# A hybrid trunk step in fp32: seven block products for the mixer's last projection and for three tile pairs of the attention's last one, and an earlier swap of a small-tile pool

## The chip, the cores and the metric

The kernel runs on one core of a Trainium2 chip. The metric is the device time of one execution in microseconds, as the median of several runs; lower is better. One further execution is recorded by the hardware profiler.

## The reference

One layer of a trunk is applied to 512 prompt tokens and 64 sample tokens with a state of their own, D = 1024, all in fp32:

```python
x = x + mixer(rmsnorm(x))        # gated delta net || gated linear attention
x = x + cross_attn(rmsnorm(x), mem_k, mem_v)
x = x + conv_ffn(rmsnorm(x))     # up, causal conv of width 3, SiLU gate, down
y = rmsnorm(x)
```

The parts that the change touches are these:

```python
merged = sigmoid(gt_a) * (o_a @ w_out_a) + sigmoid(gt_b) * (o_b @ w_out_b)
mixer  = merged @ w_o                                   # "wo"
m = rmsnorm(mem); k = m @ w_mk; v = m @ w_mv            # 256 memory tokens
a = softmax((h @ w_mq) @ k.T / 16)                      # 4 heads of 256
cross_attn = concat_heads(a @ v) @ w_mo                 # "mo"
ffn = (silu(conv(h @ w_up_gate)) * conv(h @ w_up_val)) @ w_down   # D_FF = 2816
```

The new memory keys and values, the recurrences' states and the last rows of both convolutions are outputs too.

## The kernel before

**Arithmetic.** TensorE multiplies in a reduced fp32 format. To reach fp32, weights and activations are each split into a high part and a low rest, and each block product is three matmuls: high times high, high times low, low times high. A projection tile of 128 outputs has 8 blocks of 128 inputs, and each block streams all 576 tokens (256 and 320 columns): 8 x 3 x 2 = 48 matmuls. Its accumulator is a tile `big` of two PSUM banks, of which there are two; four single banks are called `sm`.

**Weights.** SP fetches a raw tile of 512 KB (`wr`, three of them). ACT writes its rounded copy to the high tile and the negative of that to the low tile, and POOL issues a DMA that adds the raw weights to the low tile from HBM (`w<-wt`, `w<-wd` for the down projection). `fetch` prefetches in the fixed order `WORDER` as long as weight tiles `w` are free: six (`WB`) in the first part of the kernel, and six more (`WF`) from a pool `fp`.

**Order.** A planner (`Driver`) keeps a clock and a cost for each operation and writes the instructions of each engine in the order that comes out of it. All of them are issued from one line, so that the profile gives one line for nearly everything, L227, and groups go by the names of tiles. On the chip each engine takes its instructions in that order and waits on semaphores. The same order is written for PE, and prefetched weights fall into the gaps of the other engines' plans.

**Stages.** In order of PE's work: the input projections with the two recurrences in between (to about 345 us); 16 gate tiles; 8 tiles `out` (418.7 to 469.6 us), whose results are gated and merged, split into `mgh` and `mgl`; 8 tiles `wo` (469.6 to 520.4 us), each added to a tile of x that is loaded again just before; then the memory keys `mk`, values `mv` and queries `mq` with the attention of four heads; 8 tiles `mo` (the first six blocks of tiles 0 and 1 fill the last head's softmax, the rest runs from 663.8 to 705.4 us), each followed by the sum of squares and the split for the next norm; 44 tiles `up` with the convolution and gating beside them; and the down projection.

**Block products.** The down projection doesn't run as plain tiles. The 22 blocks of 128 inputs are cut into parts of six (the last of four). For a part and a pair of neighbouring output tiles, the weights are a 2 x 2 matrix of quarters, a11 to a22, and the activations (even and odd block, first and second half of the 576 tokens) another. Seven products of sums of quarters take the place of eight, in a variant of Strassen's method: P1, P2, P3, Q4, Q5, Q6, Q7. `emit_product` makes the sums of the weights (`ws`, on DVE), `operands` those of the activations (`tu`, `tw`), and `products` runs the matmuls of 288 columns into `sm` banks and adds or subtracts each result into the two halves of x by DVE. The blocks stand at 803 to 837, 915 to 948 and 1026 to 1059 us, each with four pairs; the last part follows the last `up` tile.

**Pools.** The small tiles of the recurrences live in a pool `tp`. It is closed, and `fp` opened in its place, in `main` after `mo` and before the first `up`:

```python
        drv.flush(float("inf"))
        tctx.close()
        nonlocal tp, fp
        tp = fp = ctx.enter_context(tc.tile_pool(name="fp", bufs=WF))
        drv.spawn(c_rstat("n3", [(acc, 0)], 4, True, 2.0))
```

`c_rstat` makes a norm's row factor and copies it to all partitions (`rbc`); `up` results are multiplied by it when DVE takes them out of PSUM (`fu<-big,rbc`).

Of the kernel before, what the change touches and what calls it, by code (L numbers as in the profile page):

```python
# [17 lines left out]
P = 128  # L18
# [9 lines left out]
NS = 57  # L28
RAWB = 3
WB = 6  # L30
WF = 6
# [17 lines left out]
M_ID, M_TRI, M_NEG, M_N1, M_ONE, M_GLA, M_SH, M_LEV = 0, 128, 256, 384, 512, 640, 768, 896  # L49
# [12 lines left out]
def weight_order():  # L62
    seq = list(HEADS)
    for m in range(8):
        seq += [("gta", m), ("gtb", m)]
    seq += [("out", m) for m in range(8)]
    seq += [("wo", m) for m in range(8)]
    for hd in range(4):
        seq += [("mk", 2 * hd), ("mk", 2 * hd + 1)]
        if hd % 2 == 0:  # L70
            seq += [("mv", 2 * hd + i) for i in range(4)]
        seq += [("mq", 2 * hd), ("mq", 2 * hd + 1)]
    seq += [("mo", m) for m in range(8)]
    for kd, i in FFN:
        if kd == "up":
            seq += [("up", i), ("up", NJ + i)]
        elif kd == "dns":
            seq += [("dn*", u) for u in product_order(i)]
        else:
            seq += [("dn", (m, 3)) for m in i]  # L80
    return seq
# [6 lines left out]

PRODUCTS = ("P1", "Q5", "Q6", "P2", "P3", "Q7", "Q4")


def product_order(pairs):
# [23 lines left out]
WFULL = [w for w in WORDER if w[0] not in ("dn", "dn*")]  # L116
# [79 lines left out]
class Driver:  # L196
# [32 lines left out]
    def where(self, ap):  # L229
# [4 lines left out]
        if ap.space == bass.MemoryType.PSUM:  # L234
            return ap.tensor.name, (0, P, 0, 1024)
# [20 lines left out]
    def rotate(self, tag, bufs, tile_):  # L256
# [3 lines left out]
        if len(q) >= bufs:  # L260
            end, old = self.free_at(tag)
            q.remove(old)
# [151 lines left out]
def tile_trunk(ctx, tc, xT, memT, wt, wd, vec, cst, w0, wgate, st_gdn, st_conv, st_gla, st_ffn, ckT, cv,  # L414
# [57 lines left out]
    def raw_tile():  # L472
        return keep(drv.rotate("raw", RAWB, wp.tile([P, 1024], F32, tag="raw", name=nm("wr"), bufs=RAWB)))
# [11 lines left out]
    def emit_weight(i):  # L485
        kind, idx = WORDER[i]
        if kind == "dn*":
            wready[i] = emit_product(*idx)
            return
# [23 lines left out]
    halves_of = {}  # L513

    def emit_product(pair, prod):

        m, p = pair
        n = len(PARTS[p]) * 64
        if prod == "P1":
            r = halves_of[pair] = []  # L520
            for i in range(2):
                raw = raw_tile()
                c0 = PART0[p] * 128
                src = wd[m + i, :, c0:c0 + 2 * n]
# [5 lines left out]
        def total(a, b):  # L530
            s_ = slot("ws")
            V.tensor_tensor(s_[:, 0:n], a, b, op=ALU.add)
            r.append(s_[:, 0:n])
            return s_[:, 0:n]

        src = {"P1": lambda: a11, "Q5": lambda: total(a21, a22), "Q6": lambda: total(r[4], a11), "P3": lambda: total(r[5], a12),
               "Q7": lambda: total(a11, a21), "P2": lambda: a12, "Q4": lambda: a22}[prod]()
# [7 lines left out]
        if prod in ("P2", "Q4"):  # L545
            drop(src)
# [15 lines left out]
    def fetch(i):  # L562

        room = WB + (WF if fp is not None else 0)
        for j in range(i, len(WORDER)):
            if j in wready:
                continue
            if len(drv.pending & wnames) + (1 if WORDER[j][0] == "dn*" else 2) > room:
# [12 lines left out]
    cst_t = cp.tile([P, NM], F32, name="cst")  # L581
# [12 lines left out]
    w0_t = cp.tile([P, 256], F32, name="w0")  # L594
    DMA(w0_t, w0)
    ident = cst_t[:, M_ID:M_ID + 128]
    tri = cst_t[:, M_TRI:M_TRI + 128]
    neg = cst_t[:, M_NEG:M_NEG + 128]
    negm1 = cst_t[:, M_N1:M_N1 + 128]
    ones = cst_t[:, M_ONE:M_ONE + 128]  # L600
    shift = cst_t[:, M_SH:M_SH + 128]
    glam = cst_t[:, M_GLA:M_GLA + 128]
# [8 lines left out]
    wg_t = cp.tile([P, 256], F32, name="wg")  # L611
    cst_in = cp.tile([P, 12, 3], F32, name="cstin")
    cst_out = cp.tile([P, 12, 6], F32, name="cstout")
    csamp = cp.tile([P, 12, TS], F32, name="csamp")
# [124 lines left out]
    sg = cp.tile([P, 12, 20], F32, name="sg")  # L739
# [16 lines left out]
    def c_gates(ba):  # L756
        G.memset(bt, 0.0)
        p1 = sm()
        sel = cst_t[:, M_SEL:M_SEL + 8]
# [145 lines left out]
    def c_gdn(h):  # L905
# [118 lines left out]
        for li, b in enumerate(LEVELS):  # L1024
# [10 lines left out]
            lm = cst_t[:, M_LEV + 128 * li:M_LEV + 128 * li + 128]  # L1035
# [253 lines left out]

    def c_att(hd):  # L1290
        ks_, vs_, kp_, vp_ = N["ks", hd], N["vs", hd], N["k", hd], N["v", hd]
# [45 lines left out]
        for j in range(2):  # L1337
# [15 lines left out]
        drv.done.add(("att", hd))  # L1353


    def main():
# [53 lines left out]
        DMA(cst_t, cst)  # L1410
# [88 lines left out]
        mg = []  # L1499
        for m in range(8):  # L1500
# [8 lines left out]
            h, lo = slot("mgh", F32R), slot("mgl", F32R)  # L1509
            A.copy(h[:, 0:T], g0[:, 0:T])  # L1510
            X.tensor_tensor(lo[:, 0:T], g0[:, 0:T], f(h[:, 0:T]), op=ALU.subtract)
            mg.append((h, lo))

        def res_finish(ps, m, scale, gcol, acc_, out):
            for xx, i in zip(two(x[m]), pv(ps)):
                V.scalar_tensor_tensor(xx, i, scale, xx, op0=ALU.mult, op1=ALU.add)
            out.append(norm_prep(x[m], vcol(gcol + m)))
            sq_acc(acc_, x[m], m == 0)

        acc = slot("acc")  # L1520
        out = []
        for m in range(8):
            xt = slot("x")
            DMA(xt[:, 0:T], xT[:, m, :])
            x[m] = xt
            b = []
            yield from tile_proj("wo", m, xs_of(mg), b)
            res_finish(b[0], m, 0.5, C_GMEM, acc, out)
        xs = xs_of(out)
        drv.spawn(c_rstat("n2", [(acc, 0)], 4, True, 2.0))  # L1530

        first = True
        yield ("nm",)
        N["mrt"], N["mbc"] = N["nm"]
        for hd in range(4):
            kr = slot("kraw")
            for j in range(2):
                wh, wl = weight("mk", 2 * hd + j)
                ps = big()
                for k in range(KT):  # L1540
                    a, b = N["mx"][k]
                    mm3([(ps[:, 0, 0:256], slice(0, 256))], wh, wl, a, b, k, k == 0, k == 7)
                    if k % 2:
                        yield 0.7
                V.tensor_tensor(kr[:, 256 * j:256 * j + 256], ps[:, 0, 0:256], N["mbc"][:, 0:256], op=ALU.mult)
            DMO(o_mk[256 * hd:256 * hd + 256, :].rearrange("(j p) t -> p j t", p=P), r4(kr[:, 0:512], 256))
            N["k", hd] = split(kr)
            ckr, cvr = slot("ckr"), slot("cvr")
            DMA(r4(ckr[:, 0:512], 256), ckT[:, 2 * hd:2 * hd + 2, :])
            DMA(r4(cvr[:, 0:512], 256), cv[:, 256 * hd:256 * hd + 256].rearrange("(a p) d -> p a d", p=P))  # L1550
            N["ks", hd], N["vs", hd] = split(ckr), cvr
            if hd % 2 == 0:
                nh = hd // 2
                vr = [slot("vraw") for _ in range(2)]
                ps = big()
                for kp in range(4):
                    wh, wl = weight("mv", nh * 4 + kp)
                    for tt in range(2):
                        c = slice(128 * tt, 128 * tt + 128)
                        for k in range(2):  # L1560
                            a, b = N["mx"][2 * kp + k]
                            w1, w2 = wh[:, 512 * k:512 * k + 512], wl[:, 512 * k:512 * k + 512]
                            PE.matmul(ps[:, tt, :], a[:, c], w1, start=(kp == 0 and k == 0), stop=False)
                            PE.matmul(ps[:, tt, :], a[:, c], w2, start=False, stop=False)
                            PE.matmul(ps[:, tt, :], b[:, c], w1, start=False, stop=(kp == 3 and k == 1))
                            yield 1.0
                for tt in range(2):
                    for j in range(2):
                        A.activation(vr[j][:, 256 * tt:256 * tt + 256], ps[:, tt, 256 * j:256 * j + 256],
                                     AF.Identity, scale=N["mrt"][:, tt:tt + 1])  # L1570
                for j in range(2):
                    DMO(o_mv[:, 256 * (hd + j):256 * (hd + j) + 256].rearrange("(a p) d -> p a d", p=P), r4(vr[j][:, 0:512], 256))
                    N["v", hd + j] = split(vr[j])
            for j in range(2):
                m = 2 * hd + j
# [413 lines left out]
```

## Time and profile before

| | |
|---|---|
| median of 3 runs | 1142.08 us (1141.47 to 1143.43) |
| the profiled execution | 1141.34 us, span 1139.5 us |
| 8 tiles `wo` | 469.6 to 520.4 us |
| `mo` after the last head | 663.8 to 705.4 us |
| first `up` tile | from 705.4 us |
| DMA | 172.53 MB, mean 151 GB/s |

The page gives for each engine its busy time, the share of the span and the number of instructions. A row of a group gives line, engine, operation, tiles written and read, count, busy time, mean nanoseconds of one, and the idle time before them with what ended it. A row of the timeline gives start, duration, engine, operation, and in brackets the idle time ahead of it. A row of the chain of waits gives start, duration, engine and tile.

### The profile page before, as it was taken

The numbers are of one execution on the slowest core, as the hardware profiler recorded it, in microseconds if no ns is written. First come the engines' busy times: TensorE is split into PE (matmuls) and PEld (weight loads), VectorE is DVE, ScalarE is ACT, GpSimd is POOL, SyncE is SP. The second block draws the span as 40 slices with busy tenths as digits, with TensorE's granted clock in tenths as the row PEclk, the third lists the DMA queues.
The fourth block names the chain that finished last, engine by engine and source line by source line (L and its number), as shares of the span: only waits on it lengthen the run. The fifth ranks groups of instructions, "written<-read, shape, count | busy, mean of one in ns | idle before, by whom it ended". The sixth has DMA issues, their size and how long they took to land.

```text
span 1139.5 us, 21399 instructions
## 1 busy us (share of the span) xinstructions
PE 1117.0 (98%) x8453; PEld 1076.4 (94%) x8453; DVE 628.7 (55%) x1296; ACT 618.3 (54%) x1138; POOL 294.8 (26%) x540
## 2 busy tenths in 40 slices
PE   8999999999999999999999999899999999999997
PEld 7899989998889999999999999899999999999987
DVE  6777646555533135345563443467835773677475
ACT  6766437554534354454545555654646555656554
POOL 4244114521311131111001011324423342343332
PEclk9999999999999999999999999999999999999999
DMA  8665334654336678885836846974697579848834
GB/s 259 149 144 126 63 79 89 153 121 101 80 65 166 173 171 199 224 178 141 230 120 156 205 110 156 230 181 74 141 257 178 100 165 224 208 73 189 189 68 122
DMA packets 61557, 172.53 MB, mean 151 GB/s; under 512 B 7056, under 2 KB 19600, under 8 KB 61456
## 3 DMA queue, kind: packets, MB, share of 16 engines
q0 software_dynamic: 25632, 73.41, 37.8%
q1 hardware_dynamic: 35824, 97.74, 26.2%
q8 instruction: 67, 1.10, 0.4%
q14 instruction: 34, 0.28, 0.1%
HBM read 163.13 MB, written 5.37 MB: 148 GB/s over the span
## 4 chain that ended last, share of the span: by engine, by line
PE 93%; DVE 3%; ACT 2%; DMA 1%; issue 0%; SPq 0%; POOL 0%; ACTq 0%
PE big L227 70%; PE sm L227 22%; DMA wr<-wt 1%; ACT w L227 1%; DVE x L227 1%; DVE fc L227 0%; DVE c L227 0%; SPq L227 0%; ACT xh L227 0%; DVE acl L227 0%; ACT sq L227 0%; DVE xl L227 0%; DVE gy L227 0%; DVE w L227 0%; DVE gna L227 0%
## 5 line engine op out<-in xcount | busy, mean ns | idle before, releaser
L227 PE MATMUL big<-xh,w 128*128 128x256 f32 (+1 forms) x3072 | 554.8, 300 | 6.7 <-DMA wr<-wt 3.9
L227 PEld LDWEIGHTS big<-xh,w 128*128 128x128 f32 x3072 | 463.1, 189 | 13.1 <-issue 8.8
L227 PE MATMUL big<-xl,w 128*128 128x256 f32 (+1 forms) x1536 | 330.3, 297 | 1.8 <-DVE xl L227 1.8
L227 PEld LDWEIGHTS big<-xl,w 128*128 128x128 f32 x1536 | 259.2, 190 | 2.4 <-DVE xl L227 2.4
L227 POOL DMA_DIRECT2D w<-wt x118 | 103.3, 882 | 445.4 <-ACT w L227 411.9
L227 ACT ACTIVATE w<-wr 128x1024 fp32r<-128x1024 f32 (+3 forms) x164 | 148.6, 906 | 109.8 <-PE big L227 52.9
L227 ACT CAST w<-wr 128x1024 fp32r<-128x1024 f32 (+3 forms) x184 | 164.3, 894 | 42.7 <-issue 21.4
L227 PE MATMUL sm<-ach,w 128*128 128x288 f32 (+1 forms) x496 | 103.4, 297 | 5.4 <-DVE x L227 5.4
L227 PEld LDWEIGHTS sm<-ach,w 128*128 128x128 f32 x496 | 80.9, 188 | 7.5 <-DVE x L227 6.7
L227 DVE TENSOR_TENSOR fu<-big,rbc 128x512 f32<-128x512 f32 x88 | 36.2, 454 | 92.4 <-PE big L227 84.0
L227 DVE SCALAR_TENSOR_TENSOR fc<-fu,vec,fc 128x578 f32<-128x578 f32 x88 | 71.1, 818 | 9.7 <-ACT fc L227 9.3
L227 ACT ACTIVATE fc<-fu,vec 128x578 f32<-128x578 f32 x44 | 38.2, 871 | 68.3 <-DVE fu L227 68.3
L227 PE MATMUL sm<-acl,w 128*128 128x288 f32 (+1 forms) x248 | 68.4, 295 | 0.0
L227 POOL COPY fout<-fu 128x2 f32<-128x2 f32 x88 | 34.9, 427 | 123.4 <-DVE fu L227 123.2
L227 DVE TENSOR_TENSOR x<-x,sm 128x288 f32<-128x288 f32 (+1 forms) x100 | 43.7, 449 | 30.0 <-PE sm L227 29.8
L227 POOL DMA_DIRECT2D w<-wd x46 | 40.9, 915 | 69.0 <-ACT w L227 68.9
L227 PEld LDWEIGHTS sm<-acl,w 128*128 128x128 f32 x248 | 46.7, 188 | 0.0
L227 PE MATMUL big<-aoh,w 128*128 128x256 f32 (+1 forms) x256 | 45.1, 296 | 0.0
L227 PE MATMUL big<-oh,w 128*128 128x256 f32 (+1 forms) x256 | 44.9, 296 | 0.0
L227 PE MATMUL big<-mgh,w 128*128 128x256 f32 (+1 forms) x256 | 44.6, 295 | 0.0
L227 PEld LDWEIGHTS big<-oh,w 128*128 128x128 f32 x256 | 38.5, 188 | 0.3 <-DMA w<-wt 0.3
L227 PEld LDWEIGHTS big<-mgh,w 128*128 128x128 f32 x256 | 38.7, 189 | 0.0
(331 smaller groups left out, 1770.6 us busy)
## 6 DMA issues: line engine op xcount, KB each, us to landing
wr<-wt SPq DMA_DIRECT2D x134, 512.0 KB, 5.7
w<-wt POOLq DMA_DIRECT2D x118, 512.0 KB, 7.2
wr<-wd SPq DMA_DIRECT2D x24, 384.0 KB, 3.6
w<-wd POOLq DMA_DIRECT2D x36, 192.0 KB, 4.2
x<-xT SPq DMA_DIRECT2D x16, 288.0 KB, 6.1
w<-ws POOLq DMA_DIRECT2D x12, 192.0 KB, 4.0
wr<-wd SPq DMA_DIRECT2D x8, 256.0 KB, 3.0
o_y<-yo SPq DMA_DIRECT2D x8, 256.0 KB, 3.0
```

The source lines that it names most:

```text
L227: fn(*args, **kw)
```

## The change

- **`wo`**: eight tiles become four pairs of seven products, each of 12 matmuls of 288 columns (four pairs of blocks, three terms). The merged gates stay in fp32, and `c_wo_operands` makes the sums of the activations while `out` still runs. The weights of a pair are packed with even blocks first.
- **`mo`**: tiles 2 to 7 become three pairs of seven products. Tiles 0 and 1 stay plain. Each head's result is copied to a fp32 tile `ao`, then split, and `operands` makes the sums at the end of `c_att`.
- **Order**: `mk` 0 and the first half of `mv` run before `wo`, the second half of `mv` and `mk` 1 behind it, and then `mq` and the other `mk` in turn. All eight tiles of x are loaded again at the end of `out`. The norm behind `wo` is done by chains `c_norm`.
- **Pools**: `swap_pools` runs at the recurrences' end, before `out`. `WF` goes from 6 to 3; one raw tile more (`RF`) and the eight tiles of x lie in `fp`. `NS`, the number of common slots, goes from 57 to 55. Some tiles that only the recurrences use move from the lasting pool to `tp`, and the constants come in two DMAs.
- **Products** use the two banks of a `big` tile and one `sm` bank for P2. The order of the last pair is P1, Q5, Q4 of the pair before, Q6, P3, Q7, P2, Q4. Sums of weights are made once and kept, and raw tiles are freed at the last use. The planner follows PSUM by banks.
- **FFN order**: the last pair of the third part (tiles 6 and 7) moves from the block behind it to the place behind the last `up` tiles, ahead of tiles 0 and 1 of the last part.

By instruction counts, 84 matmuls fewer (48 in `wo`, 36 in `mo`), and 92 more instructions on DVE, 73 on ACT, 18 on POOL.

```diff
-NS = 57
+NS = 55
 RAWB = 3
 WB = 6
-WF = 6
+WF = 3
+RF = 1
...
+WPAIRS = [(("wo", m), ("wo", m + 1)) for m in range(0, 8, 2)]
+ATT = [("mk", 0), ("mv", 0), ("wo", 0), ("mv", 1), ("mk", 1), ("mq", 0), ("mq", 1), ("mk", 2), ("mq", 2), ("mk", 3), ("mq", 3)]
+MPAIRS = [(("mo", m), ("mo", m + 1)) for m in range(2, 8, 2)]
...
-        late = [("dns", [(m, p) for m in range(0, 8, 2)])]
-    return seq + [("dn", (0, 1)), ("dns", [(2, 3), (4, 3)]), ("dn", (6, 7))]
+        pairs = [(("dn", (m, p)), ("dn", (m + 1, p))) for m in range(0, 8, 2)]
+        late = [("dns", pairs if p < 2 else pairs[:3])]
+        if p == 3:
+            seq.append(("dns", [(("dn", (6, 2)), ("dn", (7, 2)))]))
+    return seq + [("dn", (0, 1)), ("dns", [(("dn", (m, 3)), ("dn", (m + 1, 3))) for m in (2, 4)]), ("dn", (6, 7))]
...
     seq = []
     for i, pair in enumerate(pairs):
-        seq += [(pair, "P1"), (pair, "Q5")]
+        last = i == len(pairs) - 1
+        now = [(pair, p) for p in (("P1", "P2", "Q5", "Q6", "Q7") if whole else
+                                   ("P1", "Q5", "Q6", "P3", "Q7", "P2", "Q4") if last else ("P1", "Q5", "Q6", "P2", "P3", "Q7"))]
         if i:
-            seq.append((pairs[i - 1], "Q4"))
-        seq += [(pair, p) for p in ("Q6", "P2", "P3", "Q7")]
-    return seq + [(pairs[-1], "Q4")]
+            now.insert(2, (pairs[i - 1], "Q4"))
...
     def raw_tile():
+        if fp is not None and (len(drv.ring.get("rawf", ())) < RF or drv.free_at("rawf") < drv.free_at("raw")):
+            return keep(drv.rotate("rawf", RF, fp.tile([P, 1024], F32, tag="rawf", name=nm("wr"), bufs=RF)))
...
-            h, lo = slot("aoh", F32R), slot("aol", F32R)
+            o = slot("ao")
             for c, reg in ((slice(0, TP), pp), (slice(TP, T), p64[:, 0:64])):
-                A.copy(h[:, c], reg)
-                V.tensor_tensor(lo[:, c], reg, f(h[:, c]), op=ALU.subtract)
-            ao[2 * hd + j] = (h, lo)
+                A.copy(o[:, c], reg)
+            yield [o]
+            ao[2 * hd + j] = hl2(o)
...
+        mops[hd] = yield from operands(*os_, None, *ao[2 * hd:2 * hd + 2])
...
+    def products(pairs, ops, finish, whole=False):
+        ab, cc = {}, {}
+        for pair, prod in product_order(pairs, whole):
+            if prod == "P1":
+                ab[pair] = big()
+            if prod == "P2":
+                cc[pair] = sm()
+            a, b = ab[pair][:, 0, 0:HT], ab[pair][:, 1, 0:HT]
+            c = cc[pair][:, 0:HT] if pair in cc else None
+            o = b if prod in ("Q5", "P3") else c if prod == "P2" else a
+            start = prod in ("P1", "Q5", "P2")
+            wh, wl = weight("*", (pair, prod), False)
...
+            finish(pair, prod, a, b, c)
+            drop(wh)
+            fetch(wpos[0])
...
-        mem_prep()
         yield tuple([("oa", h) for h in range(5)] + [("ob", p) for p in range(2)])
+        swap_pools()
...
+            elif kd == "wo":
+                yield tuple(("wops", m) for m in range(1, 8, 2))
+                yield from products(WPAIRS, [wops[m] for m in range(1, 8, 2)], wo_finish)
+                drv.done.add("wo")
...
+        yield (("mops", 3),)
+        yield from products(MPAIRS, [mops[hd] for hd in range(4)], mo_finish)
...
-        drv.flush(float("inf"))
-        tctx.close()
-        nonlocal tp, fp
-        tp = fp = ctx.enter_context(tc.tile_pool(name="fp", bufs=WF))
```

More of the change, by code (lines that the diff above doesn't have):

```diff
@@ L544, in emit_product @@
             X.tensor_tensor(lo, src, f(h), op=ALU.subtract)
-        if prod in ("P2", "Q4"):
-            drop(src)
+        u = used.setdefault(pair, set())
+        u |= {prod} | set(sums)
+        for a, ps in ((a11, {"P1", "s2", "s3", "s4", "P2"}), (a22, {"s1", "s3", "Q4"})):
+            if ps <= u:
+                drop(a)
         return h, lo
@@ L580, in tile_trunk @@
     vec_t = cp.tile([P, NV], F32, name="vec")
[L581 removed]
+    keep_t = cp.tile([P, 256], F32, name="keep")
+    cst_t = tp.tile([P, NM - 256], F32, tag="cst", name="cst", bufs=1)
     DMA(vec_t, vec)
@@ L1352, in c_att, with parts2, hl @@
+            os_.append(o)
             yield
         drv.done.add(("att", hd))
+        mops[hd] = yield from operands(*os_, None, *ao[2 * hd:2 * hd + 2])
+        drv.done.add(("mops", hd))
+    N1, N2 = slice(0, HT), slice(HT, T)
+    def parts2(h, lo, src):
+        A.copy(h, src)
+        X.tensor_tensor(lo, src, f(h), op=ALU.subtract)
+    def hl(src, new=None):
+        t_ = (new or slot)("hl", F32R)
+        h, lo = t_[:, 0:HT], t_[:, HT:T]
+        parts2(h, lo, src)
+        return h, lo
@@ L1356, in main, with swap_pools, xslot @@
+    def swap_pools():
+        nonlocal tp, fp
+        tctx.close()
+        tp = fp = ctx.enter_context(tc.tile_pool(name="fp", bufs=WF))
+    def xslot(i, s="x"):
+        return drv.rotate(f"F{i}", 1, fp.tile([P, SLOT], F32R if s != "x" else F32, tag=f"F{i}", name=nm(s), bufs=1))
     def main():
@@ L1508, in main @@
             X.tensor_tensor(g0[:, 0:T], g0[:, 0:T], g1[:, 0:T], op=ALU.add)
[L1509 to L1518, printed above, removed]
+            if m % 2:
+                drv.spawn(c_wo_operands(m, gates[2 * m - 2], g0))
@@ L1520, in main, with c_wo_operands @@
+        def c_wo_operands(m, ce, co):
+            yield [ce, co]
+            wops[m] = yield from operands(ce, co)
+            drv.done.add(("wops", m))
+        mem_prep()
+        for m in range(8):
+            yield from out_tile(m)
+        for m in range(8):
+            x[m] = xslot(m)
+            DMA(x[m][:, 0:T], xT[:, m, :])
+        yield ("nm",)
+        N["mrt"], N["mbc"] = N["nm"]
         acc = slot("acc")
         out = []
[L1522 to L1575, printed above, removed]
-                b = []
-                yield from tile_proj("mq", m, xs, b)
-                if first:
-                    first = False
-                    yield ("n2",)
-                    use_norm("n2")
-                q = slot("q")
-                evac(b[0], two(q))
-                h, lo = slot("qh", F32R), slot("ql", F32R)
-                A.copy(h[:, 0:T], q[:, 0:T])
-                X.tensor_tensor(lo[:, 0:T], q[:, 0:T], f(h[:, 0:T]), op=ALU.subtract)
-                N["q", m] = (h, lo)
-            drv.spawn(c_att(hd))
@@ new lines, in wo_finish @@
+        def wo_finish(pair, prod, a, b, c):
+            m = pair[0][1]
+            xx, scale = (x[m], 0.5) if prod in ("P1", "Q6", "P3", "P2") else (x[m + 1], -0.5)
+            half = N1 if prod in ("P1", "P2", "Q4") else N2
+            V.scalar_tensor_tensor(xx[:, half], b if prod in ("Q5", "P3") else c if prod == "P2" else a, scale, xx[:, half],
+                                   op0=ALU.mult, op1=ALU.add)
+            if prod == ("P2" if m == 6 else "P3"):
+                drv.spawn(c_norm(m, C_GMEM, acc, out))
+            elif prod == "Q4":
+                drv.spawn(c_norm(m + 1, C_GMEM, acc, out))
@@ new lines, in c_norm @@
+        def c_norm(m, gcol, acc_, out_):
+            yield [x[m]]
+            sq_acc(acc_, x[m], m == 0)
+            drv.done.add(("sq", m))
+            if drv.ready(*(("sq", i) for i in range(8))):
+                drv.spawn(c_rstat("n2", [(acc_, 0)], 4, True, 2.0))
+            while not drv.ready("wo"):
+                yield WAIT
+            out_.append((m, norm_prep(x[m], vcol(gcol + m))))
+            drv.done.add(("norm", gcol, m))
+        for kd, i in ATT:
+            if kd == "mk":
+                yield from mem_keys(i)
+            elif kd == "mv":
+                yield from mem_values(i)
+            elif kd == "wo":
+                yield tuple(("wops", m) for m in range(1, 8, 2))
+                yield from products(WPAIRS, [wops[m] for m in range(1, 8, 2)], wo_finish)
+                drv.done.add("wo")
+            else:
+                if i == 0:
+                    yield tuple(("norm", C_GMEM, m) for m in range(8))
+                    xs = xs_of([p for _, p in sorted(out, key=lambda t: t[0])])
+                ckr, cvr = slot("ckr"), slot("cvr")
+                DMA(r4(ckr[:, 0:512], 256), ckT[:, 2 * i:2 * i + 2, :])
+                DMA(r4(cvr[:, 0:512], 256), cv[:, 256 * i:256 * i + 256].rearrange("(a p) d -> p a d", p=P))
+                N["ks", i], N["vs", i] = split(ckr), cvr
+                for m in (2 * i, 2 * i + 1):
+                    b = []
+                    yield from tile_proj("mq", m, xs, b)
+                    if m == 0:
+                        yield ("n2",)
+                        use_norm("n2")
+                    q = slot("q")
+                    evac(b[0], two(q))
+                    h, lo = slot("qh", F32R), slot("ql", F32R)
+                    A.copy(h[:, 0:T], q[:, 0:T])
+                    X.tensor_tensor(lo[:, 0:T], q[:, 0:T], f(h[:, 0:T]), op=ALU.subtract)
+                    N["q", m] = (h, lo)
+                drv.spawn(c_att(i))
@@ L1697, in operands, with inner @@
+        def inner(ke, ko, ce, co, whole):
             if whole:
-                fe, fo = full[ke], full[ko]
-                o.update({"P1": cut(fe, N1), "P2": cut(fo, N1), "P3": cut(fo, N2)})
-            else:
-                fo = full.pop(ko)
-                o.update({"P1": full.pop(ke), "P2": cut(fo, N1), "P3": cut(fo, N2)})
+                o = yield from operands(ce, co, None, full[ke], full[ko])
+            else:
+                o = yield from operands(ce, co, None, full.pop(ke), full.pop(ko))
@@ L1735, in last_tile, with dn_finish @@
+        def dn_finish(pair, prod, a, b, c):
+            m, p = pair[0][1]
+            xx, op = (x[m], ALU.add) if prod in ("P1", "Q6", "P3", "P2") else (x[m + 1], ALU.subtract)
+            half = N1 if prod in ("P1", "P2", "Q4") else N2
+            V.tensor_tensor(xx[:, half], xx[:, half], b if prod in ("Q5", "P3") else c if prod == "P2" else a, op=op)
+            if p == 3 and prod == "Q4":
+                last_tile(m)
+                last_tile(m + 1)
         def last_tile(m):
@@ L1761, in main @@
             elif kd == "dns":
-                yield tuple(("act", j) for j in PARTS[i[0][1]])
-                yield from products(i)
+                ks = PARTS[i[0][0][1][1]]
+                yield tuple(("act", j) for j in ks)
+                yield from products(i, [ops[k] for k in ks[0::2]], dn_finish)
             else:
```

263 lines of the change are left out of this document (155 added, 108 removed).

## The prediction

> **What bounds the kernel now.** I read the page's first and fourth parts, then the chain of waits in order of time, then the groups and the timeline where PE's work broke off.
>
> ```profile
> span 1139.5 us, 21399 instructions
> PE 1117.0 (98%) x8453; PEld 1076.4 (94%) x8453; DVE 628.7 (55%) x1296; ACT 618.3 (54%) x1138; POOL 294.8 (26%) x540
> PE 93%; DVE 3%; ACT 2%; DMA 1%; issue 0%; SPq 0%; POOL 0%; ACTq 0%
> ```
>
> TensorE sets the end: 93% of the chain is PE, and PE is idle for only 22 us of the span. So two things pay: fewer matmuls, and closing one of the few holes. The chain gives the price of a matmul and the largest hole (start, us, engine, tile):
>
> ```profile
> 433.74 93.26 PE big L227 x708
> ...
> 665.27 40.44 PE big L227 x304
> 707.94 5.69 ACT w L227 x6
> 713.64 10.82 DMA wr<-wt
> 724.47 77.99 PE big L227 x576
> 807.61 27.63 PE sm L227 x207
> 837.23 76.22 PE big L227 x576
> ```
>
> Plain projection tiles (pairs of 256 and 320 columns) take 76.22/576 = 132.3 ns a matmul, so a tile of 48 takes 6.35 us. The down projection's 288-column products take 27.63/207 = 133.5 ns. `out` and `wo` lie in the unbroken stretch from 433.74. PE's idle times, each in brackets, with the group that holds the small ones:
>
> ```profile
> 724.46 0.51 PE L227 MATMUL big<-xh,w 128*128 128x256 f32 x2 [3.91 <-DMA wr<-wt]
> 835.77 0.40 PE L227 MATMUL sm<-ach,w 128*128 128x288 f32 x1 [0.55 <-DVE x L227]
> 1102.65 0.53 PE L227 MATMUL big<-ach,w 128*128 128x256 f32 x2 [0.40 <-ACT ach L227]
> 1103.44 0.38 PE L227 MATMUL big<-acl,w 128*128 128x256 f32 x1 [0.26 <-DVE acl L227]
> 1108.39 0.40 PE L227 MATMUL sm<-ach,w 128*128 128x288 f32 x1 [1.77 <-DVE x L227]
> 1110.47 0.41 PE L227 MATMUL sm<-ach,w 128*128 128x288 f32 x1 [0.22 <-DVE x L227]
> L227 PE MATMUL sm<-ach,w 128*128 128x288 f32 (+1 forms) x496 | 103.4, 297 | 5.4 <-DVE x L227 5.4
> ```
>
> **Part 1, the products.** A pair of tiles goes from 96 matmuls of 132.3 ns (12.70 us) to 7 x 12 = 84 of 133.5 ns (11.21 us): 1.49 us saved. Four pairs of `wo` and three of `mo` give 7 x 1.49 = **-10.4**. All of it is on PE, hence on the path.
>
> **Part 2, the hole at 720.55.** Around it the timeline shows:
>
> ```profile
> 703.51 19.75 SPq L227 DMA_DIRECT2D wr<-wt  x6
> 720.92 1.06 ACT L227 ACTIVATE w<-wr 128x1024 fp32r<-128x1024 f32 x1 [4.13 <-DMA wr<-wt]
> 722.82 0.69 ACT L227 COPY rbc<-sm 128x512 f32<-128x512 f32 x2
> 723.43 1.55 DVE L227 TENSOR_TENSOR fu<-big,rbc 128x512 f32<-128x512 f32 x4 [8.33 <-ACT rbc L227]
> ```
>
> Opening the second pool before `up` frees six weight tiles at once, SP asks for six raws, and ACT stands 4.13 us before a raw that has not landed. Behind it in ACT's queue is the copy `rbc` (the norm's row factor), without which DVE cannot empty the first `up` banks; PE waits 3.91. The next 576 matmuls take 77.99 instead of 76.22, so 1.77 us more. In the change the pool is opened at the recurrences' end, four raws are in flight instead of three, and the first `up` weights are loaded behind `mo`'s products. Both go: **-5.7**. What is late next is `rbc` itself: the norm's chain may end only after x7, whose last finish now comes with the last product. From there to `rbc` I estimate 10.9 us, adding up the steps between (finish, square, sum, root, copies) with nothing in their way; the two `up` tiles whose banks are free take 2 x 6.35 = 12.7. That is 1.8 us to spare, so I put nothing here and keep +5.7 as a rival.
>
> The clock needs a word. The hole is 3.91 us of idleness, followed by 1.77 us lost in 576 matmuls. [...]
>
> **Part 3, the down products' new order.** In each block the last pair ended with two products on one bank, and PE waited for DVE (0.55 us, three times, and 0.64 near the end, out of the group's 5.4). The last pair now runs P1, Q5, Q4 of the pair before, Q6, P3, Q7, P2, Q4, which puts another product between: 3 x 0.55 + 0.64 = **-2.3**.
>
> **Part 4, the FFN's end.** Part 2's last down pair moves behind the last `up` tiles: 7 products of 9 matmuls, 63 x 133.5 ns = 8.4 us of PE work, while ACT and DVE make the last operands. That covers the four waits from 1102 to 1110, 0.40 + 0.26 + 1.77 + 0.22 = **-2.65**. The cover is needed once and is longer than the waits' 8 us from first to last.
>
> **Part 5, what the products add.** The work beside PE, by rows of the down block and of `wo`/`mo` (DVE):
>
> ```profile
> L227 DVE TENSOR_TENSOR x<-x,sm 128x288 f32<-128x288 f32 x27 | 11.8, 451 | 7.6 <-PE sm L227 7.6
> L227 DVE TENSOR_TENSOR kvl<-kraw,kvh 128x512 fp32r<-128x512 f32 x4 | 2.8, 693 | 1.4 <-ACT kvh L227 1.1
> L227 DVE TENSOR_TENSOR w<-wr,w 128x1024 fp32r<-128x1024 f32 x16 | 19.4, 1219 | 2.7 <-ACT w L227 2.3 <-PE big L227 0.4
> L227 DVE TENSOR_TENSOR acc<-acc,sq 128x576 f32<-128x576 f32 x14 | 10.5, 753 | 0.0
> L227 DVE SCALAR_TENSOR_TENSOR xl<-x,vec,xh 128x576 fp32r<-128x576 f32 x16 | 13.1, 818 | 13.2 <-ACT xh L227 13.2
> 470.00:521.00 51.00, 51.00 (x386) 51.00 (x386) 20.12 (x33) 25.14 (x30) 5.29 (x7) 1.00 0.77 185
> 663.80:705.50 41.70, 41.57 (x315) 41.34 (x314) 16.25 (x29) 23.72 (x30) 6.03 (x7) 1.00 0.69 155
> 803.00:837.00 34.00, 33.05 (x248) 32.59 (x247) 23.34 (x52) 20.73 (x36) 13.42 (x19) 1.00 0.86 199
> ```
>
> (In the last three: length, then busy PE, PEld, DVE, ACT, POOL, the clock, the DMA share, GB/s.) In the changed order DVE does during `wo`'s 44.9 us: 28 finishes (12.6 us), 21 sums and lows of 512 columns (693 ns as the 512-wide row, 14.6), 7 `acc` adds (5.3) and 4 lows of `mv` weights (4.9): 37.4, or 83%. During `mo`'s 33.6 us: 21 finishes (9.5), 16 sums and lows (11.1), 6 `acc` and 7 `xl` (10.2): 30.8, or 92%, and 23.8 of it in the first 22.4. The down block ran at 23.34 of 34 (69%). A finish may be late by one product (1.6 us) before PE notices, since another product lies between two uses of a bank. The 1.4 us by which `mo`'s first two pairs are over-full shows in part: **+1.2** (0.3 to 4, if ACT's waits are added).
>
> Three entries have no row in the trace before:
>
> - Last head to `mo`. Now `ao` is copied from PSUM to fp32 first, and split after.
>
> ```profile
> 663.90 0.70 ACT L227 CAST aoh<-sm 128x512 fp32r<-128x512 f32 x2 [1.15 <-PE sm L227]
> 664.52 0.82 DVE L227 TENSOR_TENSOR aol<-sm,aoh 128x512 fp32r<-128x512 f32 x2 [1.02 <-ACT aoh L227]
> 665.27 0.55 PE L227 MATMUL big<-aol,w 128*128 128x256 f32 x2
> ```
>
>   One ACT copy more (0.70) and its hand-over: at least 0.75. At most another such round (0.70 and 0.82 and a bank's release), 2.5: P1 waits for the banks of `mo` 0. I take **+1.6**.
> - `wo`'s start: Q5's weight is the sum of two quarters, made and reloaded before its turn, in ACT's queue behind P2's; **+0.5** (0 to 2), and pair 2's Q5 **+1.0** (0.4 to 1.4). First `up` tile behind x7's `xl`: **+0.3** (0 to 0.8, the `xl` row).
> - Nine weight tiles instead of twelve in the FFN, so weights are made three products (3.6 us) later at each end of a block:
>
> ```profile
> 823.72 1.06 ACT L227 ACTIVATE w<-wr 128x1024 fp32r<-128x1024 f32 x1
> 825.07 0.86 POOL L227 DMA_DIRECT2D w<-wt  x1 [1.32 <-ACT w L227]
> w<-wt POOLq DMA_DIRECT2D x4, 512.0 KB, 9.8
> w<-wt POOLq DMA_DIRECT2D x118, 512.0 KB, 7.2
> ```
>
>   The first `up` weight was begun at 823.72 for a use at 837.23: 13.5 us ahead, then 9.9. It needs 1.35 to the issue and 7.2 (whole run) to 9.8 us (this block) to land: 8.6 to 11.2. So between 1.3 us of slack and 1.3 us late, at three blocks: **+1.0** (0 to 3.9).
>
> Sum: -10.4 - 5.7 - 2.3 - 2.65 = -21.05; +1.2 + 1.6 + 0.5 + 1.0 + 0.3 + 1.0 = +5.6; net -15.4. The profiled execution took 1141.34 us, the median is 1142.08 (0.74 above), so **1126.7** for the median (1125.9 for a run like the profiled one). With all costs at their low ends (1.5) 1122.5, at their high ends (13.6) 1134.7.
>
> **Rivals.**
>
> *The products starve on what feeds them* (0.17). DVE at 83 to 92% with ACT's casts in between leaves little room: an in-order queue that waits once hands the delay on. 49 products that each wait 0.2 us lose 9.8 us, all but the products' gain: about 1135.3. For it: the 0.38 to 0.55 us waits `<-DVE x` that down blocks show at only 69%. Against it: those blocks lose only at their two ends, and the new order has a product between. [...]
>
> *The hole stays* (0.08): ACT still meets an unlanded raw before `rbc`, or x7's norm is later than I worked out: +5.7, 1132.4.
>
> *Nine weight tiles are too few* (0.11), the one that ends slower. Place: three block ends, and the turns from `wo` to `mv` and from `mo` to `up`, where cheap products (one tile per 1.6 or 1.2 us) give way to weights of two tiles. Price: landing time + 1.35 - 9.9 us each. It decides from 3.3 us at five places (5 x 3.3 = 16.4, the net gain with its +1.0), that is landings of 11.8 us; from about 12.5 each hole also costs the half clock's 1.77, and five of 5.8 make 1126.7 - 1.0 + 29 = 1154.7; middle 1149. For it: DMA stands at 0.86 in the block and landings reached 9.8 there, with 7.2 the median. Against it: the block's demand for bytes is unchanged and spread by later starts, and four raws replace three.
>
> *The change doesn't do what it says* (0.04): the products cost as much as the tiles, because the shared `big` banks add a wait of 0.2 us per product or the matmuls of 288 columns rise to 152 ns; -10.4 is gone: 1137.
>
> **How the numbers follow.** Forecast 0.60. Range 1120 to 1138: the low end is the costs' low end (1122.5) less 2.5 for a cheaper `mo` entry and no loss in the norm's chain; the high end takes in the high costs, the staying hole, the starving products and the last case; left out are the fourth part's slow case and a little below. A difference of 0.2% (2.3 us) is what a measurement can tell. Faster than 1139.8: the forecast, the first two rivals and the last, 0.86 after some allowance for sums of two; same 0.03; slower 0.11.
>
> **What would show it.** After: PE's busy time about 10 us less with no idle above 1 us near the start of `up` (else the hole stayed); `wo` some 45 to 47 us and `mo`'s products some 34 to 36 (more: starvation, with waits `<-DVE x` on `big`); no 0.55 waits at the ends of the down blocks; the idle from 1102 to 1110 gone; the first `up` weight after a block with a wait `<-DMA w<-wt` if nine tiles are too few. Wrong would be waits of over 3 us at the turns, or a half clock in the FFN.

## The result and the profile after

The changed kernel takes 1154.41 us (1154.1 to 1156.45) where the kernel before takes 1141.78 (1141.42 to 1143.43) on the same chip: ratio 1.0112, 95% interval 1.0094 to 1.0129. It is slower by 12.6 us; the forecast was 1126.7, with a range of 1120 to 1138.

The page of the changed kernel: its first part, the chain by engine, and from the groups the matmuls of the products (tiles, count | busy, mean ns | idle time ahead of them and what ended it).

```profile
span 1152.5 us, 21456 instructions
PE 1113.3 (97%) x8369; PEld 1063.9 (92%) x8369; DVE 692.1 (60%) x1400; ACT 645.8 (56%) x1211; POOL 306.7 (27%) x560
PE 93%; DVE 3%; DMA 1%; issue 1%; ACT 1%; SPq 0%; POOL 0%; POOLq 0%; ACTq 0%; DVEq 0%
L240 PE MATMUL big<-ach,w 128*128 128x288 f32 (+1 forms) x832 | 175.2, 299 | 13.0 <-DVE x L240 10.7
L240 PE MATMUL big<-acl,w 128*128 128x288 f32 (+2 forms) x416 | 113.4, 299 | 9.7 <-DVE x L240 9.4
```

The 84 matmuls are gone (8453 to 8369), but PE's busy time fell by 3.7 us instead of some 12, and its idle time rose from 22 to 39 us. 20.1 us of it is `<-DVE x`: the finishes, which add a product to x. Before, that group had 5.4. The hole at 720 us is gone, as forecast. The stretch that was bounded by windows before, the first down block, with PE, PEld, DVE, ACT and POOL busy, the clock, the DMA share and GB/s:

```profile
803.00:837.00 34.00, 30.69 (x219) 29.01 (x217) 23.19 (x50) 19.83 (x39) 13.60 (x19) 1.00 0.83 183
```

DVE does the same 23 us of work in these 34 us as before (23.34), and PE gets 219 matmuls done instead of 248. The block, which the change was to shorten by half a microsecond, lasts 39.2 us from its first to its last product matmul; before, 34.8. One of its holes, in the timeline of the changed kernel:

```profile
802.76 0.29 PE L240 MATMUL big<-hl,w 128*128 128x288 f32 x1
...
802.89 0.29 PE L240 MATMUL big<-ach,w 128*128 128x288 f32 x1
...
803.02 0.30 PE L240 MATMUL big<-acl,w 128*128 128x288 f32 x1
...
803.16 0.29 PE L240 MATMUL big<-ach,w 128*128 128x288 f32 x1
803.49 0.45 DVE L240 TENSOR_TENSOR x<-x,big 128x288 f32<-128x288 f32 x1
...
804.00 0.40 PE L240 MATMUL big<-acl,w 128*128 128x288 f32 x1 [0.55 <-DVE x L240]
```

The matmul at 802.76 (`hl`) is the last of P1. Three matmuls of Q5 follow (`ach`, `acl`, `ach`). DVE's finish of P1 starts when the third of them has ended, and the fourth waits until the finish has ended. Yet P1 is in the first bank of its `big` tile and Q5 in the second. Of the three matmuls the trace shows a semaphore update on the third alone; DVE's finish waits on that semaphore, and the weight load of the fourth matmul waits on DVE's. It looks as if the finish were ordered by the tile of two banks: as a read of a tile that the third matmul has written and the fourth will write. The other holes have the same form. In 34 of the 36 waits `<-DVE x` after 360 us the finish starts 0.04 us behind the end of the matmul ahead of the hole, and the next matmul 0.06 to 0.15 us behind the end of the finish. From start to start such a hole costs 0.84 us where 0.13 is the rule, 0.71 us; the 0.55 in brackets understates it, because the end of a matmul lies 0.16 us behind the start of its successor.

The holes can be summed: every time from the start of a matmul to the next start that is over 0.3 us, less the 0.133 that is the rule, after 360 us. That gives 38.9 us in the changed kernel and 16.3 in the kernel before: +22.6. Of the 10.4 us of matmul time and the 1.8 us of half clock (granted 0.50 from 726 to 729 us in the kernel before, 1.00 from 720 to 740 us in the changed one) that had to go, 3.5 came back, since the 288-column matmuls rose from 133.5 to 136.0 ns, 1428 of them. That leaves +13.9, where the span grew by 13.0; the 0.9 us between them is not accounted for.

### The profile page after: what moved, and what is told of

It reads as the page before. It is cut to its first block, busy times and chain, and to the rows that moved or that the text cites. A ratio compares the mean times of both kernels' runs of the same rounds, so it can differ in the third digit from the quotient of the medians.

```text
span 1152.5 us, 21456 instructions
## 1 busy us (share of the span) xinstructions
PE 1113.3 (97%) x8369; PEld 1063.9 (92%) x8369; DVE 692.1 (60%) x1400; ACT 645.8 (56%) x1211; POOL 306.7 (27%) x560
## 4 chain that ended last, share of the span: by engine, by line
PE 93%; DVE 3%; DMA 1%; issue 1%; ACT 1%; SPq 0%; POOL 0%; POOLq 0%; ACTq 0%; DVEq 0%
PE big L240 77%; PE sm L240 16%; DVE x L240 2%; DMA w<-wt 1%; DMA x<-xT 1%; DVE c L240 0%; SPq L240 0%; DVE xl L240 0%; DVE xi L240 0%; DVE gy L240 0%; DVE gna L240 0%; ACT vraw L240 0%; ACT gx L240 0%; ACT mh L240 0%; ACT ao L240 0%
## 5 line engine op out<-in xcount | busy, mean ns | idle before, releaser
L240 POOL DMA_DIRECT2D w<-wt x125 | 109.8, 878 | 378.5 <-ACT w L240 319.0
L240 PE MATMUL big<-ach,w 128*128 128x288 f32 (+1 forms) x832 | 175.2, 299 | 13.0 <-DVE x L240 10.7
L240 PEld LDWEIGHTS big<-ach,w 128*128 128x128 f32 x832 | 135.2, 188 | 18.8 <-DVE x L240 11.7
L240 PE MATMUL big<-acl,w 128*128 128x288 f32 (+2 forms) x416 | 113.4, 299 | 9.7 <-DVE x L240 9.4
L240 PEld LDWEIGHTS big<-acl,w 128*128 128x128 f32 x416 | 77.0, 188 | 14.0 <-DVE x L240 12.5
L240 DVE TENSOR_TENSOR fu<-big,rbc 128x512 f32<-128x512 f32 (+1 forms) x88 | 36.3, 453 | 76.1 <-PE big L240 73.1
L240 DVE TENSOR_TENSOR x<-x,big 128x288 f32<-128x288 f32 (+2 forms) x110 | 47.6, 449 | 46.4 <-PE big L240 45.7
L240 ACT CAST w<-ws 128x384 fp32r<-128x384 f32 (+2 forms) x84 | 43.5, 533 | 33.3 <-DVE ws L240 28.5
L240 DVE TENSOR_TENSOR w<-ws,w 128x384 fp32r<-128x384 f32 (+2 forms) x62 | 36.0, 591 | 14.3 <-ACT w L240 13.6
L240 DVE TENSOR_TENSOR gt<-big,rbc 128x512 f32<-128x512 f32 (+1 forms) x32 | 13.2, 451 | 45.7 <-PE big L240 45.7
```

The source lines that it names most:

```text
L240: fn(*args, **kw)
```

## The experiments

Three theories were tested. Theory A: waits are set by the tile, so two banks of one tile are one resource. Theory B: DVE is too late for the products. Theory C: nine weight tiles are too few.

**e1_banks.** The products' accumulators in single banks:

```diff
-                ab[pair] = big()
+                ab[pair] = keep(sm())
+            if prod == "Q5":
+                bb[pair] = sm()
...
-            a, b = ab[pair][:, 0, 0:HT], ab[pair][:, 1, 0:HT]
+            a = ab[pair][:, 0:HT]
+            b = bb[pair][:, 0:HT] if pair in bb else None
```

> The changed kernel, but each product's accumulators a, b and c are `sm` tiles of one bank, as before, instead of two halves of one `big` tile. Theory A (one tile, two banks: DVE's finish of a product in one bank is ordered against the matmuls of the next product in the other, because waits are set by the tile): the 26 or so PE holes of 0.55 us (0.71 us from start to start) behind a DVE finish go, about -18.5 us: near 1136 us, 1131 to 1140. Theory B (DVE is simply too late for the products, the starving rival): the finishes stay late in their queue, less than 4 us come back, above 1150 us. Theory C (nine weight tiles): no change either.

Measured: 1128.99 us (1127.96 to 1131.01), ratio to before 0.9887 [0.987, 0.9905]; 25.4 us under the changed kernel. Groups and chain of e1:

```profile
L240 PE MATMUL sm<-ach,w 128*128 128x288 f32 (+1 forms) x856 | 175.9, 297 | 3.1 <-DMA w<-ws 1.2
L240 PE MATMUL sm<-acl,w 128*128 128x288 f32 (+1 forms) x428 | 117.5, 295 | 0.0
```
```profile
669.34 33.47 PE sm L240 x252
...
714.64 79.34 PE big L240 x600
793.99 4.76 PE sm L240 x36
...
798.78 29.00 PE sm L240 x216
827.78 76.01 PE big L240 x576
```

The waits for finishes are gone, and `mo`'s 252 product matmuls run without a break in 33.47 us. DVE's work is the same, 690.1 us against 692.1, and so is the number of weight tiles: B and C fall as causes. The same place in e1's timeline, P1 (`hl`) and Q5's first matmuls:

```profile
793.82 1.34 PE L240 MATMUL sm<-hl,w 128*128 128x288 f32 x9
...
795.00 0.29 PE L240 MATMUL sm<-ach,w 128*128 128x288 f32 x1
...
795.39 0.30 PE L240 MATMUL sm<-acl,w 128*128 128x288 f32 x1
795.43 0.45 DVE L240 TENSOR_TENSOR x<-x,sm 128x288 f32<-128x288 f32 x1
795.53 0.29 PE L240 MATMUL sm<-ach,w 128*128 128x288 f32 x1
795.66 0.30 PE L240 MATMUL sm<-acl,w 128*128 128x288 f32 x1
```

The finish runs in the middle of Q5, at about the same point as in the changed kernel, and PE goes on beside it, a matmul every 0.13 to 0.14 us. In both kernels the finish reads one bank while the matmuls fill another; what differs is whether the two banks are one tile, so it is the program's waits that stop PE and not a conflict of the two engines at PSUM. I had expected 18.5 us, from 26 holes that stand `<-DVE x` at 0.71. By the sum from start to start 23.4 us of holes are gone (those of 0.64 bracketed cost 0.80, and others had a different name) and 3.5 us of spacing, together 0.9 us more than the 26.0 by which the span fell.

**e2_before_big.** The other way round, in the kernel before: the down products into the halves of a `big` tile.

```diff
-                if start:
-                    banks[bank] = sm()
-                o = banks[bank][:, 0:HT]
+                if prod == "P1":
+                    banks[pair] = big()
+                if prod == "P2":
+                    o = sm()[:, 0:HT]
+                else:
+                    o = banks[pair][:, 1 if prod in ("Q5", "P3") else 0, 0:HT]
```

> The kernel before, with nothing changed but the down products' accumulators: a and b are the two halves of a `big` tile instead of two `sm` banks. Theory A: some five more holes of 0.71 us in each of four groups of products, 10 to 16 us slower, 1152 to 1158 us. Theory B and C: DVE's load and the weight tiles are as before, so within 2 us of the kernel before.

Measured: 1179.87 us, ratio 1.0336 [1.031, 1.0361]: +37 us, with no other change. The sign is A's, the size is over twice what I expected: the first block grew from 34.8 to 45.1 us. Its groups, and the first two holes of a block by windows (busy PE is the first figure after the length, the granted clock the third from the right):

```profile
L227 PE MATMUL big<-ach,w 128*128 128x288 f32 (+1 forms) x464 | 107.2, 311 | 29.0 <-DVE x L227 26.1
```
```profile
805.00:808.50 3.50, 1.83 (x12) 1.37 (x11) 3.34 (x8) 2.72 (x5) 0.93 (x3) 1.00 0.37 55
808.50:812.50 4.00, 3.15 (x13) 3.15 (x14) 2.67 (x6) 0.65 (x3) 1.55 (x2) 0.57 0.57 133
```

There are ten holes to a block, where the changed kernel has seven. At the start of the first block PE is busy for 1.83 of 3.5 us, and the granted clock is 0.57 in the 4 us behind them.

**e10_after_whole.** The planner's part in it. The change also made the planner follow PSUM by banks; here it follows tiles again, and the products stay in `big`.

```diff
-            return ap.tensor.name, (0, P, lo // 512 * 512, (hi + 511) // 512 * 512)
+            return ap.tensor.name, (0, P, 0, 1024)
```

> The changed kernel, with its products in two halves of a `big` tile, and only the planner's PSUM tracking by whole tiles as before. It tells what the planner has to do with it. Theory A (the hardware's waits are set by the tile in any case): the planner now knows and puts each finish behind its product, the next product of the same tile still waits for it, 2 to 3 holes a pair instead of 1 to 3: 1150 to 1165, no better than the change. If only the planner's belief in free banks makes the holes: near e1, 1130.

Measured: 1177.2 us, ratio 1.0306 [1.0289, 1.0324], above what I expected.

```profile
L240 PE MATMUL big<-ach,w 128*128 128x288 f32 (+1 forms) x832 | 182.1, 302 | 40.9 <-DVE x L240 36.8
```

A planner that knows of the shared tile puts the whole finish between the two products, and PE waits for more (36.8 us in this group instead of 10.7). The planner by banks hides part of that, but can't take the wait away. The first down block takes 44.6 us here and took 45.1 in e2, whose planner follows whole tiles too.

**e4_whole.** The same line put back in e1, where the products have banks of their own.

> e1_banks with one line of the planner as before: it takes a PSUM tile as a whole again, not bank by bank. In e1 the four evacuations of `mv` (ACT, vraw) are still put among the last matmuls of the other bank of the same `big` tile: PE holes of 0.56 us `<-ACT vraw`, and short ones beside them, some 3 us in all. Theory A (waits are set by the tile, and the planner by banks writes an order that runs into them): they go, -2 to -3 us against e1, about 1126.3. If the holes come from ACT's load: no change, 1129.

Measured: 1125.7 us (1125.26 to 1126.79), ratio 0.986 [0.9845, 0.9875], the lowest median of all and 3.3 us under e1. The holes that it removed stand in e1's timeline:

```profile
489.37 0.51 PE L240 MATMUL big<-w,mh 128*128 128x512 f32 x1 [0.56 <-ACT vraw L240]
...
548.37 0.50 PE L240 MATMUL big<-w,mh 128*128 128x512 f32 x1 [0.56 <-ACT vraw L240]
...
549.67 0.50 PE L240 MATMUL big<-w,mh 128*128 128x512 f32 x1 [0.56 <-ACT vraw L240]
```

ACT empties one bank of `mv`'s tile while PE's last matmuls go to the other. In e4's trace none of the three is left. This is the same mechanism at a place that I had not looked at: the planner believed the bank free and wrote an order that runs into the tile's wait.

**e3_before_order.** The kernel before with the two new orders only, parts 3 and 4:

```diff
+        seq += [(pair, p) for p in (("Q6", "P3", "Q7", "P2") if i == len(pairs) - 1 else ("Q6", "P2", "P3", "Q7"))]
...
+        late = [("dns", [(m, p) for m in range(0, 8 if p < 2 else 6, 2)])]
+        if p == 3:
+            seq.append(("dns", [(6, 2)]))
```

> The kernel before with the two orders of the change alone: the last pair as P1, Q5, Q4 of the pair before, Q6, P3, Q7, P2, Q4, and the third part's last pair behind the last `up` tiles. Parts 3 and 4 of the prediction: -2.3 and -2.65, so 1137 us (1136 to 1139). If the holes at the block ends or from 1102 to 1110 us come back elsewhere: 1140 to 1142.

Measured: 1142.02 against 1142.67, ratio 0.9998 [0.9989, 1.0007]: nothing. PE's waits in two stretches of it:

```profile
916.88 0.40 PE L229 MATMUL sm<-ach,w 128*128 128x288 f32 x1 [1.02 <-DVE x L229]
920.10 0.40 PE L229 MATMUL sm<-ach,w 128*128 128x288 f32 x1 [0.58 <-DVE x L229]
934.88 0.37 PE L229 MATMUL sm<-ach,w 128*128 128x288 f32 x1 [0.23 <-DVE x L229]
```
```profile
1094.49 0.37 PE L229 MATMUL sm<-ach,w 128*128 128x288 f32 x1 [0.56 <-DVE x L229]
1097.63 0.37 PE L229 MATMUL sm<-ach,w 128*128 128x288 f32 x1 [0.49 <-ACT w L229]
1112.02 0.41 PE L229 MATMUL sm<-ach,w 128*128 128x288 f32 x1 [1.00 <-DVE x L229]
```

The holes at the blocks' ends are gone, but ones of 1.02 and 0.58 us stand at the starts of two of them, where one of 0.38 stood before, and of the end's 2.65 us, 2.05 are back at other places. PE's idle time between its first and last matmul is 15.6 us, before 15.7. In e1, with the rest of the change around them, the three blocks' products do take less, 33.8, 33.6 and 25.8 + 8.35 us instead of 34.8, 34.8 and 34.9; what else in the change clears their starts wasn't tried.

**e6_wo_plain and e7_mo_plain.** e1 with `wo`, or with `mo`, as eight plain tiles and without the sums of operands:

```diff
-            seq += [("*", u) for u in product_order(WPAIRS)]
+            seq += [("wo", m) for m in range(8)]
```

> e1_banks with `wo` as eight plain tiles (and no sums of its operands): by the prediction the products of `wo` are worth 4 x 1.49 = 5.95 us less 1.5 for their start and second pair and about 0.5 of waits: +4 us, 1133. If the products are fully free of waits: +6, 1135. If what feeds them costs as much as they save: 1129 or less.

> e1_banks with `mo` as eight plain tiles (no sums of operands per head): by the prediction 3 x 1.49 = 4.5 us less 1.6 for the entry and 0.7 of waits: +2.2 us, 1131. If the products are free of waits: +4.5, 1133.5. If feeding them costs as much: 1129 or less.

Measured: 1133.43 and 1132.73 us against e1's 1128.99, so the products of `wo` are worth 4.4 us and those of `mo` 3.7. These are differences between runs on two chips, and e1's own runs lie 3 us apart; by the ratios to the kernel before they are 4.7 and 3.8. Both were forecast a little too low (4 and 2.2): in e1 the products take 45.8 and 33.5 us, and feeding them shows little.

**e9_slow_room.** The kernel before, with the six weight tiles of the late pool given to the prefetch two at a time:

```diff
-        room = WB + (WF if fp is not None else 0)
+        room = WB + min(WF, max(0, 2 * (wpos[0] - WORDER.index(("up", 0)) - 2)))
```

> The kernel before, but after the pool's late opening the prefetch is given the six new weight tiles two at a time, one pair for each `up` weight used, not at once. By part 2 of the prediction (the burst of raws holds ACT ahead of `rbc`) the hole of 3.91 us and the half clock behind it go: -5.7, 1136.4 (1135.5 to 1138). If the norm's chain itself is late, or the missing prefetch opens new holes among the first `up` tiles: 1140 to 1143.

Measured: 1138.07 against 1142.74, ratio 0.9962 [0.9947, 0.9977]: -4.7 us. The chain goes through the place of the hole without a break; the four `sm` matmuls are the norm's own:

```profile
665.19 45.21 PE big L227 x340
710.40 0.99 PE sm L227 x10
711.39 5.47 PE big L227 x40
716.86 0.80 PE sm L227 x4
717.65 79.09 PE big L227 x596
```

The burst of raws was the cause of the hole, and one line of the prefetch is enough to be rid of it. The 1.0 us that is missing to the 5.7 can be found at the start of the first down block, where e9's trace has waits of 1.05 and 0.57 us `<-DVE x` and the kernel before had one of 0.40.

**e8_ten_tiles, e11_mem_early, e12_slow_room.** Three trials to improve on e4, one edit each:

```diff
-WF = 3
+WF = 4
...
+        mem_prep()
         yield tuple([("oa", h) for h in range(5)] + [("ob", p) for p in range(2)])
         swap_pools()
...
-        mem_prep()
...
-        room = WB + (WF if fp is not None else 0)
+        room = WB + min(WF, max(0, wpos[0] - WORDER.index(("out", 0)) - 2))
```

> e4_whole with one weight tile more in the late pool (ten instead of nine). In e1 the last products wait for weights that land late (1.17 and 0.29 us for accumulates, 0.94 for ACT, near 1100 us). If nine tiles are the cause (the third rival, in small): -1 to -2.5 us against e4, about 1124.5. If the landing itself is: no change.

> e4_whole with the memory's preparation (four loads and their split) ahead of the pool's opening, as in the kernel before. In e4 the hole of 1.65 us at 433 us `<-DMA w<-wt` stands behind eight raws asked for at once (six before). If the preparation's loads in that burst are its cause: -1.5, 1124.2. If the burst of weights alone is: 1125.7, no change.

> e4_whole with e9's edit at the new place of the pool's opening: the three weight tiles of the late pool are given to the prefetch one by one, one for each `out` weight used. The hole of 1.65 us at 433 us `<-DMA w<-wt` stands behind a burst of raws and accumulates. If the burst is its cause: -1 to -1.8, 1124. If the fourth raw tile alone makes it, or the weights come too late now: 1125.7 to 1127.

Measured: 1126.28, 1127.97 and 1127.27 us. None is faster than e4: the first lies within its scatter, the others are 1.6 to 2.3 us above it, but on other chips, and e12's interval overlaps e4's. With ten tiles the holes near 1100 us do go, and new ones open, of 0.73 us in `wo` (`<-DMA w<-wt`) and of 1.34 us at the start of `up` (`<-DVE fu`). The hole of 1.65 us at 433 us (`<-DMA w<-wt`) stays in e12 (1.71): spreading the burst doesn't remove it, and what makes it stays open. e4 remains the version to take: 16.3 us under the kernel before.

## Why the prediction was wrong

**The step that failed** is a clause of part 5, which part 3 uses too: "A finish may be late by one product (1.6 us) before PE notices, since another product lies between two uses of a bank." That held in e1, where the banks are tiles of their own and `mo`'s 252 product matmuls run without a break; in `big` tiles, PE waited 0.71 us from start to start for a finish that came three matmuls behind its product (803.49), and the waits cost 25.4 us in all (e1). I had read that the products use the two banks of a `big` tile, and took the bank for the unit of waiting because the planner in the change does. Its nearest relative stood among the rivals as part of a case of 0.04, "the shared `big` banks add a wait of 0.2 us per product", priced for the 49 new products only. The size was about right (25.4 us over all 147 products is 0.17 each); that it also reaches the 98 products of the down projection, which ran well before, is what turned a gain into a loss.

- Part 1, -10.4: right. e6 and e7 give 8.1 us net of what feeds the products, where the prediction's terms make 6.2, with the scatter said above.
- Part 2, -5.7: right in its mechanism, 4.7 by e9. The margin of 1.8 us for `rbc` held: no hole opened there.
- Part 3, -2.3: the new order gives nothing alone (e3), though the three blocks take 2.9 us less in e1. Its reason fell in the changed kernel, where a block is 4.4 us longer.
- Part 4, -2.65: wrong. In e1 the last pairs wait 1.17, 0.29 and 0.94 us for weights in place of the 2.65: the cover was there, and what came late next was the weights of the products behind it. With a tenth weight tile (e8) these waits are gone.
- Part 5: the finishes' load cost nothing in `mo` (+1.2 forecast, 252 matmuls in 33.47 us). The last head's entry cost two short waits of 0.24 and 0.26 us in e1 (+1.6 forecast), and the products of `wo` waited 0.10 and 0.14 us for weights (+0.5 and +1.0). The high ends of its terms add up to 14.6, not 13.6; the range to 1138 still covered that. Missing was the evacuation of `mv`: 3.3 us (e4).
- The starving rival: DVE's load was below the count, 34.6 us in `wo` and 26.6 in `mo` in e1 where 37.4 and 30.8 had been counted, and it starves nothing. The sign that the prediction gave for starvation did come: in the changed kernel the products of `wo` take 50.9 us and those of `mo` 36.9, with waits `<-DVE x` on `big`. It could not tell a late DVE from a shared tile; e1 could, as DVE does the same work there. Nine weight tiles: no wait at the blocks' ends in e1, where `up` runs in 79.34 and 76.01 us unbroken; they show only near the end. The half clock that this rival adds from landings of 12.5 us on, that is from holes of 3.95 us (12.5 + 1.35 - 9.9), has only the one hole of 3.91 us in the kernel before behind it (granted clock 0.50 from 726 to 729 us). That it takes a hole of such a length, no run shows; in e2 the granted clock was 0.57 behind holes of 0.76 and 1.75 us. The slow side was reached by another way than the one I priced.

That e4 comes within 1 us of the forecast owes something to luck, to errors that cancel: part 4's 2.65 us didn't come and the hole at 433 us was in no term, while the costs of part 5 were set too high.

## What to carry to other kernels

Ask of each PSUM tile what the unit of its waits is. Here it is the tile (25.4 us between the changed kernel and e1): two accumulators that are filled and emptied in turn belong in two tiles, even if each has its own bank; a planner that believes otherwise writes an order that stalls (3.3 us between e1 and e4). And if a hole is filled by moving work, name the next operation whose input has not arrived: in e3 the work that closed 2.65 us at the end met 2.05 us of other waits.

## What the runs showed of the hardware that was not expected

A granted clock under 1.00 came behind shorter holes, too, than the one of 3.91 us in the kernel before. In e2's first block, holes of 0.76 and 1.75 us within 4 us, with PE busy 1.83 of 3.5 us, were followed by a granted clock of 0.57 (808.5 to 812.5 us). The same 1.7 us hole near 45 us, with PE busy 1.30 of 3 us, is followed by a granted clock of 1.00 in e1 and of 0.57 in e11 (0.59 in e2; in the other ten of the thirteen traces it is 1.00 from 47 to 51 us); e1 first:

```profile
44.00:47.00 3.00, 1.30 (x10) 1.09 (x9) 2.84 (x10) 2.99 (x6) 0.85 (x3) 1.00 0.33 64
47.00:51.00 4.00, 4.00 (x33) 4.00 (x32) 3.32 (x7) 3.42 (x8) 1.84 (x3) 1.00 0.38 133
```
```profile
44.00:47.00 3.00, 1.30 (x11) 1.10 (x10) 2.73 (x9) 2.99 (x7) 1.08 (x3) 1.00 0.24 46
47.00:51.00 4.00, 4.00 (x22) 4.00 (x21) 3.43 (x6) 3.39 (x7) 1.65 (x2) 0.57 0.41 138
```

33 matmuls fit into the second stretch in the one and 22 in the other: 4 us at 0.57 are, as an estimate, some 1.7 us lost (4 x 0.43), which come and go with no change in the code at that place. They may be a part of the scatter between runs; one trace of each kernel can't show it.
